# A hybrid decoder layer: conditioning pieces placed by columns given to TensorE, a third score buffer, later attention products

## The chip, the cores and the metric

The kernel runs on one core of a Trainium2 chip. The metric is the device time of one execution in microseconds (us). TensorE is called PE, VectorE DVE, ScalarE ACT, GpSimd POOL and SyncE SP. DMA transfers are issued by SP and POOL.

## The reference

One layer of a decoder on x (512 tokens by 2048), with a conditioning vector c of 2048 that is turned into 24 vectors of 512 values each (scales, shifts and gates):

```
mod = c_act @ wm                               # 24 groups of 512 columns, 2048 deep
h = rms_norm(x) * (1 + scale1) + shift1
h @ w_in -> group A: windowed attention, 16 query heads, 2 key/value heads, bias, sinks
            group B: 16 heads over 256 latent values; keys chosen per query by a ReLU indexer, top 128
x += gate1 * (concat(out_A, out_B) @ w_out)
h = rms_norm(x) * (1 + scale2) + shift2
x += gate2 * W_down(silu(causal_dwconv3(W_u h)) * (W_g h))       # 5632 wide
out = rms_norm(x)
```

Everything is float32.

## The kernel before

Activations lie transposed, features on 128 partitions and 512 tokens along a row. A float32 product is made of three passes in a shorter format: weights and activations are split into a high part (ACT, L129) and a low part (DVE, L130), and `mm3` (L133 to L136) gives TensorE high by high, high by low and low by high. Each 128 x 128 block of weights is thus three matmuls of 512 columns.

The projections are cut into *units* of 128 output columns, and a unit into four *slots* of 128 x 512 weights, which are 12 matmuls. `drive` (L315 to L329) goes through the slots: it starts loads five slots ahead on SP, splits three ahead, gives the slot's matmuls, and then calls `step` (L249). A step advances every active Python generator to its next `yield`, so that their work lies between the slots. Something that was put on the list `middle` is run by `run_middle` (L243) in the middle of the next slot's matmuls, or at the start of the next step. The order in which Python gives instructions sets priorities; the framework then puts each engine's stream in an order of its own by these and by its estimates, and each engine works its stream off in that order, waiting where an input is not there.

The stages, in the time of the trace: 0 to 190 us keys, values and index projection; 190 to 360 the units qa0 to qa7 (queries of group A) with the indexer, the top-k (L641 to L649: names gt, isc, cnt, wk) and pairs of A heads; 360 to 575 the units qb0 to qb7 (queries of B) with pairs of B heads; 575 to 796 the output projection, units wo0 to wo15, with x loaded in four parts of 1 MB (x2, used at L908); 796 to 2212 the gated MLP.

*A pair of heads* (`pair_gen`) goes step by step: score matmuls into PSUM (sca, scb), the bias and row minimum on DVE (L726, into a tile s, from a tag with two buffers), exp on ACT (L728), the division (`norm`), then `turns(p)`, which transposes four 128 x 128 blocks of each head into a bank (tag tp, two banks; L748) and copies it to et on ACT (L749), and `product(p)` (L762), which multiplies et by the values. A head of A has two such parts, one of B three. Before each pair of B heads, `prep_gen` makes keys from a 128 x 256 slice of wuk (names wuk0h/l to wuk7h/l): matmuls into kbp, which takes one of the two tp banks until `dup_k` (L563 to L566) has copied it to kb with two ACT and two DVE operations.

*Conditioning.* Groups 0 to 7 of mod come first. The rest is done by `mod_gen`: a *piece* is a 256 KB load and one DVE operation on 128 x 512 values that adds a row block times c to macc (L183). After 16 pieces, four small matmuls (mps, L193) sum macc over partitions, and the bias is added a step later (L230). Groups 8 to 13 run beside qb, four pieces a step, with five buffers, loaded by POOL; 14 to 19 beside wo, three a step, eight buffers, loaded by POOL (L1238); 20 to 23 beside the MLP, two a step, five buffers, loaded by SP.

Of the kernel before, what the change touches and what calls it, by code (L numbers as in the profile page):

```python
# [8 lines left out]
F32 = mybir.dt.float32  # L9
# [24 lines left out]
def hybrid_trunk(ctx, tc, xT, cT, wm, bm, nrm, wik, wiq, wi1, sinks, kvn, wuk, wuv, rel, onehot,  # L34
# [3 lines left out]

    const = ctx.enter_context(tc.tile_pool(name="const", bufs=1))
# [202 lines left out]

    def run_middle():  # L243
        todo = list(middle)
        middle.clear()
        for f in todo:
            f()

    def step():  # L249
        run_middle()  # L250
        for group in (active, idle):
            for g in list(group):
                if next(g, StopIteration) is StopIteration:
                    group.remove(g)

    def finish_all():
        while active or idle or middle:
            step()
# [56 lines left out]
    def drive(slots, lo, hi):  # L315
        for i in range(lo, hi):
# [4 lines left out]
            if middle:  # L321
                slots[i].mm(slots[i].w, range(2))
                run_middle()
                slots[i].mm(slots[i].w, range(2, 4))
            else:
                slots[i].mm(slots[i].w)
# [329 lines left out]
    ka = p1.tile([P, 4, T], F32R, name="ka")  # L656
# [29 lines left out]


    class Head:
# [10 lines left out]

        def load(self):  # L700
            self.nt = self.tb_src.shape[-1]
            self.tb = p1.tile([P, T], F32, tag="tb", bufs=2, name=f"tb{self.name}")
            sp.dma_start(self.tb[:, :self.nt], self.tb_src)

        def scores(self):
            name, spans = self.name, self.spans
            s = self.s = p1.tile([P, 1280], F32, tag="s", bufs=2, name=f"s{name}")
# [44 lines left out]
    def pair_gen(heads, o_of, done):  # L752
# [23 lines left out]
        middle.append(lambda: turns(1))  # L776
        yield
        product(0)
        product(1)
        if len(heads[0].parts) > 2:  # L780
            turns(2)
            middle.append(lambda: (product(2), done()))
            yield
        else:
            done()
# [414 lines left out]
    drive(slots, 0, marks["qb0"] - 4)  # L1200
    start(prep_gen(0))
    drive(slots, marks["qb0"] - 4, marks["qb0"])
    while idle:
        step()
    start(mod_gen(range(8, 14), ring_mod, 5, p1, sc_ps, 4), low=True)
    drive(slots, marks["qb0"], marks["wo"])
# [12 lines left out]
    for i in range(6):  # L1219
# [3 lines left out]
        drive(slots, marks["wo"] + i, marks["wo"] + i + 1)  # L1223
# [17 lines left out]
    start(mod_gen(range(14, 20), px_mod, 8, px, o_bank, 3), low=True)  # L1241
    at = marks["wo"] + 6
    for i in range(1, 4):
        n = (1,1,4)[i - 1]
        drive(slots, at, at + n)
        sp.dma_start(env["x2"][i], xT[i])
        at += n
    drive(slots, at, marks["ff"])
# [20 lines left out]
    start(mod_gen(range(20, 24), ring_mod, 5, p2, o_bank, 2), low=True)  # L1269
# [97 lines left out]
```

## Time and profile before

| | us |
|---|---|
| median of 3 runs | 2205.24 (2204.67 to 2207.21) |
| profiled execution, its own time | 2213.56 |
| its span, first to last instruction | 2211.8 |
| PE busy | 2149.8 (97%) |
| DVE busy | 1567.8 (71%) |
| ACT busy | 975.8 (44%) |
| POOL busy | 242.2 (11%) |

The profile is of one execution. Busy time counts matmuls, element-wise operations and the like, not waits. Bracketed at the end of a row of the timeline is the idle time of that engine before the row and what ended it. The granted clock (PEclk) is a share of TensorE's full 2.4 GHz; it is at full or at half of that, and a value between is a mean. An x and a number is the count of instructions in a row.

### The profile page before, as it was taken

The page shows a single profiled execution, that of the slowest core. Times are in us where ns is not written, and L with a number is a line of the kernel's source. Part 1 is how long each engine was busy: PE and PEld are TensorE (multiplying, and loading weights), DVE is VectorE, ACT ScalarE, POOL GpSimd, SP SyncE. Part 2 cuts the span into 40 slices and gives each one's busy share as a digit, 9 for nine tenths or more (in the row PEclk, how much of TensorE's full clock was granted, in tenths as well). Part 3 has the DMA queues.
Part 4 walks back from the last instruction along what each step waited for, and adds up shares of the span by engine and source line. Part 5 has one row for each costly group of instructions (what it writes and reads, how often), then busy time and mean ns, then how long its engine had stood idle before and what let it go on. Part 6 is the DMA issues. An engine that isn't in the chain of part 4 may idle for free.

```text
span 2211.8 us, 30173 instructions
## 1 busy us (share of the span) xinstructions
PE 2149.8 (97%) x10376; PEld 1752.7 (79%) x10376; DVE 1567.8 (71%) x2829; ACT 975.8 (44%) x1850; POOL 242.2 (11%) x376
## 2 busy tenths in 40 slices
PE   8999999998989999999999999999999999999997
PEld 4777777777768888888888888888888888888887
DVE  2887999787679576975757676665857666675766
ACT  4334876676722263434333343334333343334332
POOL 0000000222034000000101010110201010110200
PEclk9999999999999999999999999999999999999999
DMA  9783321666499436744737465564727465563672
GB/s 384 271 288 113 107 72 56 201 219 212 151 359 343 150 127 189 253 148 120 161 95 169 113 147 133 133 145 118 163 92 166 119 140 140 131 148 114 120 251 77
DMA packets 168921, 367.09 MB, mean 166 GB/s; under 512 B 20159, under 2 KB 27343, under 8 KB 162624
## 3 DMA queue, kind: packets, MB, share of 16 engines
q1 hardware_dynamic: 130208, 270.81, 37.3%
q0 software_dynamic: 37696, 92.79, 19.9%
q8 instruction: 81, 1.33, 0.2%
q10 hardware_dynamic: 864, 1.57, 0.2%
q14 instruction: 72, 0.59, 0.1%
HBM read 312.93 MB, written 52.17 MB: 165 GB/s over the span
## 4 chain that ended last, share of the span: by engine, by line
PE 72%; issue 17%; DMA 5%; POOL 2%; DVE 2%; ACT 1%; SPq 0%; POOLq 0%; DVEq 0%; ACTq 0%
PE p L1053 6%; PE p L1055 6%; PE p L1054 6%; DMA mraw<-in_wm_dram 4%; POOL mraw L1238 1%; POOL mraw L123 1%; PE qip L134 1%; PE mrow L188 1%; PE qip L135 1%; PE qip L136 1%; DMA xn<-in_xT_dram 0%; DVE macc L183 0%; PE mps L193 0%; DMA wiq<-in_wiq_dram 0%; PE cT L1105 0%
## 5 line engine op out<-in xcount | busy, mean ns | idle before, releaser
L169 ACT CAST dh<-rq 128x512 fp32r<-128x512 f32 x240 | 149.5, 623 | 182.9 <-PE p L1055 145.5
L183 DVE SCALAR_TENSOR_TENSOR macc<-mraw,cact,macc 128x512 f32<-128x512 f32 x240 | 179.6, 748 | 26.2 <-DMA mraw<-in_wm_dram 22.5
L170 DVE TENSOR_TENSOR dl<-rq,dh 128x512 fp32r<-128x512 f32 x240 | 160.9, 686 | 43.8 <-ACT dh L169 42.9
L1053 PE MATMUL p<-dh,ah 128*128 128x512 f32 x480 | 187.0, 390 | 0.0
L1055 PE MATMUL p<-dh,al 128*128 128x512 f32 x480 | 186.9, 389 | 0.0
L1054 PE MATMUL p<-dl,ah 128*128 128x512 f32 x480 | 186.9, 389 | 0.0
L1064 POOL DMA_DIRECT2D cd<-co x72 | 61.4, 858 | 875.0 <-DVE co L1077 872.6
L1053 PEld LDWEIGHTS p<-dh,ah 128*128 128x128 f32 x480 | 90.2, 188 | 18.7
L1054 PEld LDWEIGHTS p<-dl,ah 128*128 128x128 f32 x480 | 90.1, 188 | 18.7
L1055 PEld LDWEIGHTS p<-dh,al 128*128 128x128 f32 x480 | 90.1, 188 | 18.7
L123 POOL DMA_DIRECT2D mraw<-in_wm_dram x96 | 51.6, 538 | 357.6 <-DVE macc L181 131.1
L1080 DVE TENSOR_TENSOR v<-p,v 128x512 f32<-128x512 f32 x120 | 82.3, 686 | 6.0 <-PE p L1055 5.2
L1064 POOL DMA_DIRECT2D cd<-v x72 | 61.4, 856 | 128.1 <-DVE v L1082 76.1
L1238 POOL DMA_DIRECT2D mraw<-in_wm_dram x96 | 51.4, 536 | 133.4 <-DVE nmb L726 53.7
L170 DVE TENSOR_TENSOR al<-cu,ah 128x256 fp32r<-128x256 f32 (+2 forms) x60 | 46.7, 779 | 23.9 <-ACT ah L169 21.2
L169 ACT CAST ah<-cu 128x256 fp32r<-128x256 f32 (+2 forms) x60 | 41.5, 692 | 49.4 <-DVE cu L979 25.9
L1077 DVE TENSOR_TENSOR co<-p,v 128x512 f32<-128x512 f32 x80 | 54.9, 686 | 6.7 <-PE p L1055 6.7
L999 DVE TENSOR_TENSOR rq<-rq,rq 128x512 f32<-128x512 f32 x80 | 52.4, 684 | 0.0
L479 DVE TENSOR_TENSOR qi<-qi,qip 128x512 f32<-128x512 f32 x56 | 38.3, 684 | 14.4 <-PE qip L136 13.7
L170 DVE TENSOR_TENSOR dl_t<-tw,dh_t 128x512 fp32r<-128x512 f32 x40 | 27.7, 692 | 22.9 <-ACT dh_t L169 22.9
L728 ACT ACTIVATE sb<-sb,nmb 128x512 f32<-128x512 f32 (+2 forms) x64 | 35.3, 552 | 13.3 <-DVE nmb L726 13.0
L378 DVE SCALAR_TENSOR_TENSOR macc<-mraw,cact,macc 128x512 f32<-128x512 f32 x54 | 40.3, 746 | 0.4
(4498 smaller groups left out, 6447.5 us busy)
## 6 DMA issues: line engine op xcount, KB each, us to landing
mraw<-in_wm_dram POOLq DMA_DIRECT2D x192, 256.0 KB, 5.6
rq<-in_wdn_dram SPq DMA_DIRECT2D x160, 256.0 KB
mraw<-in_wm_dram SPq DMA_DIRECT2D x32, 1024.0 KB
cd<-co POOLq DMA_DIRECT2D x80, 256.0 KB, 4.6
cd<-v POOLq DMA_DIRECT2D x80, 256.0 KB, 4.6
mraw<-in_wm_dram SPq DMA_DIRECT2D x64, 256.0 KB
wiq<-in_wiq_dram SPq DMA_DIRECT2D x32, 256.0 KB
wik<-in_wik_dram SPq DMA_DIRECT2D x8, 592.0 KB
```

The lines of the kernel that those rows point to most:

```text
L123: by.dma_start(t, src)
L169: act.copy(hi_t, full)
L170: dve.tensor_tensor(lo_t, full, hi_t.bitcast(F32), OP.subtract)
L183: dve.scalar_tensor_tensor(acc, t, cact[:, kt:kt + 1], acc, OP.mult, OP.add)
L999: dve.tensor_tensor(self.b[out], self.b[a], self.b[b], OP.add)
L1053: pe.matmul(ps[b], ah[:, tok], wh, start=k == 0, stop=False)
L1054: pe.matmul(ps[b], ah[:, tok], wl, start=False, stop=False)
L1055: pe.matmul(ps[b], al[:, tok], wh, start=False, stop=k == 1)
L1064: pool.dma_start(cd[tb][dq], t, accum_op=OP.add)
L1077: dve.tensor_tensor(t, ps, box["v" if i == 1 else "u", b], OP.subtract)
L1080: dve.tensor_tensor(box["v", b], ps, box["v", b], OP.add)
L1238: pool.dma_start(t, wm[g, kt // 4][:, kt % 4])
```

## The change

A wrapper, `Counted`, takes TensorE's place in the kernel and adds up, while the program is built, the columns of each matmul and transpose (four times as many for float32 data, half for outputs on 64 partitions). `pace` puts a generator on a list with a number of columns, and `run_paced`, called at the end of each step and, with `halves=True`, in the middle of each slot, advances it once for each such number that TensorE has been given. `mod_gen` now yields after each piece. The numbers are 5200 for groups 8 to 13, 3500 for 14 to 19 and 20000 for 20 to 23. `finish_all` gives what is left of a paced generator at once.

`Head.third` lets every third B head use ka's buffer (A's keys, free by then) for its tile s, beside the two buffers of tag s. In `pair_gen`, the last product of an A pair moves to the middle of the following slot; for a B pair the second transposes move from the middle of a slot to behind the first product, the second product and the third transposes to the middle of the next slot, and the third product one step on. As the wrapper gives all matmuls of the changed kernel, they have its line (L53, transposes L57) in the orders below.

```diff
--- before.py
+++ after.py
@@ -36,6 +36,27 @@
     nc = tc.nc
     act, dve, pe, pool, sp = nc.scalar, nc.vector, nc.tensor, nc.gpsimd, nc.sync
 
+    class Counted:
+
+        def __init__(self, to):
+            self.to, self.cols = to, 0
+
+        def count(self, out, x):
+            n = 1
+            for d in out.shape[1:]:
+                n *= d
+            n = 4 * n + 22 if x.dtype == F32 else n + 32
+            self.cols += n // 2 if out.shape[0] == 64 else n
+
+        def matmul(self, out, w, x, **kw):
+            self.count(out, x)
+            return self.to.matmul(out, w, x, **kw)
+
+        def transpose(self, out, x, eye):
+            self.count(out, x)
+            return self.to.transpose(out, x, eye)
+
+    pe = Counted(pe)
     const = ctx.enter_context(tc.tile_pool(name="const", bufs=1))
     ring = ctx.enter_context(tc.tile_pool(name="ring", bufs=1))
     big = ctx.enter_context(tc.tile_pool(name="big", bufs=1))
@@ -240,6 +261,19 @@
             yield from gen
         (idle if low else active).append(run())
 
+    paced = []
+
+    def pace(gen, every):
+        paced.append([gen, every, pe.cols])
+
+    def run_paced(all_of=False):
+        for e in list(paced):
+            while all_of or pe.cols >= e[2]:
+                e[2] += e[1]
+                if next(e[0], StopIteration) is StopIteration:
+                    paced.remove(e)
+                    break
+
     def run_middle():
         todo = list(middle)
         middle.clear()
@@ -252,8 +286,10 @@
             for g in list(group):
                 if next(g, StopIteration) is StopIteration:
                     group.remove(g)
+        run_paced()
 
     def finish_all():
+        run_paced(True)
         while active or idle or middle:
             step()
 
@@ -312,15 +348,16 @@
 
         return [Slot(raw, s, mm(s), (lambda: after(box["ps"])) if s == 3 else None) for s in range(4)]
 
-    def drive(slots, lo, hi):
+    def drive(slots, lo, hi, halves=False):
         for i in range(lo, hi):
             for j in range(i, min(i + AHEAD_LOAD + 1, len(slots))):
                 slots[j].load()
             for j in range(i, min(i + AHEAD_SPLIT + 1, len(slots))):
                 slots[j].split()
-            if middle:
+            if halves:
                 slots[i].mm(slots[i].w, range(2))
                 run_middle()
+                run_paced()
                 slots[i].mm(slots[i].w, range(2, 4))
             else:
                 slots[i].mm(slots[i].w)
@@ -653,7 +690,7 @@
     ch = p1.tile([P, 2, T], F32R, name="ch")
     cl = p1.tile([P, 2, T], F32R, name="cl")
     va = p1.tile([P, NB, P], F32, name="va")
-    ka = p1.tile([P, 4, T], F32R, name="ka")
+    ka = p1.tile([P, 4, T], F32R, tag="ka", bufs=1, name="ka")
     wit = tmp_t("wit", (16, T))
     dup_k(ki_ps[0:64], 0, ki[:, 0], ki[:, 1])
     act.mul(wit, ki_ps[64:80], 1.0 / 32.0)
@@ -684,6 +721,8 @@
             split_to(ch[:, i], cl[:, i], cf[i])
         yield
 
+    turn_s = [0]
+
 
     class Head:
 
@@ -697,6 +736,13 @@
             self.parts = [jobs[g:g + 4] for g in range(0, len(jobs), 4)]
             self.ets = {}
 
+        def third(self):
+
+            if len(self.parts) < 3:
+                return False
+            turn_s[0] += 1
+            return turn_s[0] % 3 == 0
+
         def load(self):
             self.nt = self.tb_src.shape[-1]
             self.tb = p1.tile([P, T], F32, tag="tb", bufs=2, name=f"tb{self.name}")
@@ -704,7 +750,11 @@
 
         def scores(self):
             name, spans = self.name, self.spans
-            s = self.s = p1.tile([P, 1280], F32, tag="s", bufs=2, name=f"s{name}")
+            if self.third():
+                s = p1.tile([P, 1280], F32, tag="ka", name=f"s{name}", padded_shape=[P, 4 * T])
+            else:
+                s = p1.tile([P, 1280], F32, tag="s", bufs=2, name=f"s{name}")
+            self.s = s
             nm = p1.tile([P, NB], F32, tag="nm", bufs=3, name=f"nm{name}")
             den = self.den = p1.tile([P, NB], F32, tag="den", bufs=3, name=f"den{name}")
             banks, used, where = [], [], [None] * NB
@@ -773,15 +823,19 @@
         heads[1].norm()
         yield
         turns(0)
-        middle.append(lambda: turns(1))
-        yield
-        product(0)
-        product(1)
-        if len(heads[0].parts) > 2:
-            turns(2)
-            middle.append(lambda: (product(2), done()))
+        if len(heads[0].parts) == 2:
+            middle.append(lambda: turns(1))
+            yield
+            product(0)
+            middle.append(lambda: (product(1), done()))
             yield
         else:
+            yield
+            product(0)
+            turns(1)
+            middle.append(lambda: (product(1), turns(2)))
+            yield
+            product(2)
             done()
 
     mixa = {}
@@ -1197,13 +1251,13 @@
 
     start(ahead(index_gen(), 0))
     start(ahead(keys_gen(), 0))
-    drive(slots, 0, marks["qb0"] - 4)
+    drive(slots, 0, marks["qb0"] - 4, True)
     start(prep_gen(0))
-    drive(slots, marks["qb0"] - 4, marks["qb0"])
+    drive(slots, marks["qb0"] - 4, marks["qb0"], True)
     while idle:
         step()
-    start(mod_gen(range(8, 14), ring_mod, 5, p1, sc_ps, 4), low=True)
-    drive(slots, marks["qb0"], marks["wo"])
+    pace(mod_gen(range(8, 14), ring_mod, 5, p1, sc_ps, 1), 5200)
+    drive(slots, marks["qb0"], marks["wo"], True)
     env["mh"] = mh = big.tile([P, KT, T], F32R, tag="b2", name="mh")
     env["ml"] = ml = big.tile([P, KT, T], F32R, tag="b3", name="ml")
 
@@ -1220,7 +1274,7 @@
         if i < 3:
             for kt in range(4 * i, 4 * i + 4):
                 mix_in(kt)
-        drive(slots, marks["wo"] + i, marks["wo"] + i + 1)
+        drive(slots, marks["wo"] + i, marks["wo"] + i + 1, True)
     finish_all()
     for kt in range(12, 16):
         mix_in(kt)
@@ -1238,14 +1292,14 @@
         pool.dma_start(t, wm[g, kt // 4][:, kt % 4])
         return t
 
-    start(mod_gen(range(14, 20), px_mod, 8, px, o_bank, 3), low=True)
+    pace(mod_gen(range(14, 20), px_mod, 8, px, o_bank, 1), 3500)
     at = marks["wo"] + 6
     for i in range(1, 4):
         n = (1,1,4)[i - 1]
-        drive(slots, at, at + n)
+        drive(slots, at, at + n, True)
         sp.dma_start(env["x2"][i], xT[i])
         at += n
-    drive(slots, at, marks["ff"])
+    drive(slots, at, marks["ff"], True)
     finish_all()
 
     rs_ps = norm_rows("rs2")
@@ -1266,7 +1320,7 @@
     pxc.__exit__(None, None, None)
     pdc = tc.tile_pool(name="ph4", bufs=1, reuse_waits="tile")
     env["pd"] = pdc.__enter__()
-    start(mod_gen(range(20, 24), ring_mod, 5, p2, o_bank, 2), low=True)
+    pace(mod_gen(range(20, 24), ring_mod, 5, p2, o_bank, 1), 20000)
     drive(slots, marks["ff"] + 12, marks["join"])
     pdc.__exit__(None, None, None)
     env["pe"] = pe2 = ctx.enter_context(tc.tile_pool(name="ph5", bufs=1, reuse_waits="tile"))
```

Each engine has as many instructions as before, of the same kinds and shapes, and POOL's are in the same order. Three places, before and then changed.

The first is on DVE, between the last unit of qa and qb0. isc, gt, cnt and wk (L641 to L646, now L678 to L683) belong to the top-k, sa (L726, now L776) to a head of A, and qb0r_3l is the low half of the weights of qb0's last slot:

```order
L738 RECIPROCAL dena_3601<-dena_3601 128x4
L641 TENSOR_SCALAR gt_3724,cnt_3723<-isc_1632,top_2825 128x512
L130 TENSOR_TENSOR qb0r_3l<-qb0r_3409,qb0r_3h 128x512
L642 TENSOR_SCALAR isc_1632<-isc_1632,top_2825 128x512
L643 TENSOR_SCALAR cnt_3723<-cnt_3723 128x1
L130 TENSOR_TENSOR qb1r_0l<-qb1r_3478,qb1r_0h 128x512
L644 SCALAR_TENSOR_TENSOR wk_2826<-isc_1632 128x512
L130 TENSOR_TENSOR qb1r_1l<-qb1r_3733,qb1r_1h 128x512
L646 SCALAR_TENSOR_TENSOR isc_1632<-wk_2826,cnt_3723,isc_1632 128x512
```

In the changed kernel the same stretch, up to the row behind qb0r_3l:

```order
L679 TENSOR_SCALAR isc_1632<-isc_1632,top_2825 128x512
L680 TENSOR_SCALAR cnt_3715<-cnt_3715 128x1
L776 ISA sa_3637,nma_3638<-sca_1_3645,tba_3548,nsink 128x256
L776 ISA nma_3638 128x1
L681 SCALAR_TENSOR_TENSOR wk_2826<-isc_1632 128x512
L776 ISA sa_3637,nma_3638<-sca_1_3645,tba_3548,nsink 128x128
L776 ISA nma_3638 128x1
L683 SCALAR_TENSOR_TENSOR isc_1632<-wk_2826,cnt_3715,isc_1632 128x512
L151 TENSOR_TENSOR qb0r_3l<-qb0r_3401,qb0r_3h 128x512
L787 TENSOR_TENSOR dena_3639<-dena_3639,esa_3658 128x4
```

qb0r_3l stood behind gt; it now stands behind the chain of gt, isc, cnt and wk up to the second isc, and no split stands between these any more.

The second is on PE in the unit qb2: the transposes of a B pair into tp banks (tpb_0 the first part, tpb_1 the second) and its first product, o from etb. Before:

```order
L134 MATMUL qb2ps<-h1h,qb2r_1h 128x512
L748 MATMUL tpb_0_4101<-identr,sb_3978 128x128 x4
L748 MATMUL tpb_1_4136<-identr,sb_3914 128x128 x4
L135 MATMUL qb2ps<-h1l,qb2r_1h 128x512
L748 MATMUL tpb_1_4143<-identr,sb_3978 128x128 x4
L136 MATMUL qb2ps<-h1h,qb2r_1l 128x512
L762 MATMUL o_4156<-etb_0_4095,vb_3531 64x128
```

Changed, first the transposes of the first part and what follows them:

```order
L53 MATMUL qb2ps<-h1h,qb2r_1l 128x512
L57 MATMUL tpb_0_4049<-identr,sb_3938 128x128 x4
L53 MATMUL qb2ps<-h1h,qb2r_1h 128x512
L53 MATMUL qb2ps<-h1l,qb2r_1h 128x512
L53 MATMUL qb2ps<-h1h,qb2r_1l 128x512
L53 MATMUL o_4084<-etb_0_4043,vb_3531 64x128
```

Seven products on, the end of the first product and what follows it:

```order
L53 MATMUL o_4084<-etb_0_4050,vb_3531 64x128
L57 MATMUL tpb_1_4093<-identr,sb_3882 128x128 x4
L57 MATMUL tpb_1_4100<-identr,sb_3938 128x128 x4
L53 MATMUL scb_0_4110<-kb_4003,qb_4018 128x512
L53 MATMUL scb_0_4110<-keep_3731,identr 128x512
```

The second part's transposes stood directly behind those of the first, two banks one after the other; they now come behind three more matmuls and the first product, and the scores of the next head (scb) follow them.

The third is on DVE at the slice wuk6, whose low half wuk6l the kbp matmuls need; macc is a piece of conditioning, sb belongs to a head's scores. In the kernel before:

```order
L726 ISA sb_5400,nmb_5401<-scb_1_5407,tbb_5261 128x128
L726 ISA nmb_5401 128x1
L183 SCALAR_TENSOR_TENSOR macc_0_5359<-mraw_10_5435,cact,macc_0_5359 128x512
L183 SCALAR_TENSOR_TENSOR macc_0_5359<-mraw_11_5438,cact,macc_0_5359 128x512
L130 TENSOR_TENSOR wuk6l<-wukr_5352,wuk6h 128x256
L738 RECIPROCAL denb_5402<-denb_5402 128x4
L183 SCALAR_TENSOR_TENSOR macc_0_5359<-mraw_12_5480,cact,macc_0_5359 128x512
```

In the changed kernel, with the head's scores in the rows ahead:

```order
L776 ISA sb_5225,nmb_5226<-scb_1_5232,tbb_5174 128x384
L776 ISA nmb_5226 128x1
L776 ISA sb_5225,nmb_5226<-scb_1_5232,tbb_5174 128x128
L776 ISA nmb_5226 128x1
L788 RECIPROCAL denb_5227<-denb_5227 128x4
L151 TENSOR_TENSOR wuk6l<-wukr_5250,wuk6h 128x256
```

Two pieces stood between the scores and wuk6l, and now none. The pieces of group 13 lay in this unit; those of group 12 now lie in the next one, most of them ahead of wuk7l.

## Rows read from the trace of the kernel before

**Rows 1.** The page: the span, and busy time by engine.

```profile
span 2211.8 us, 30173 instructions
...
PE 2149.8 (97%) x10376; PEld 1752.7 (79%) x10376; DVE 1567.8 (71%) x2829; ACT 975.8 (44%) x1850; POOL 242.2 (11%) x376
```

**Rows 2.** Stretches: their length, then each engine's busy time, clock, DMA share, GB/s.

```profile
360.00:560.00 200.00, 181.00 (x1108) 146.79 (x1107) 155.47 (x356) 135.03 (x326) 40.79 (x76) 0.95 0.58 183
560.00:640.00 80.00, 69.28 (x395) 56.19 (x394) 57.25 (x113) 46.44 (x105) 12.29 (x23) 0.95 0.70 245
640.00:740.00 100.00, 98.65 (x435) 80.94 (x436) 86.98 (x139) 25.49 (x41) 38.62 (x72) 0.96 0.88 309
740.00:800.00 60.00, 58.40 (x285) 48.78 (x284) 25.68 (x42) 20.64 (x32) 0.00 (x0) 0.99 0.36 119
800.00:2130.00 1330.00, 1330.00 (x5907) 1101.88 (x5906) 900.51 (x1426) 519.61 (x841) 131.44 (x160) 1.00 0.57 146
```

**Rows 3.** Waits of PE, 360 to 800 us: in total, times, longest.

```profile
PE tpb L748 <- ACT etb L749: 9.1, 6, 3.4
PE mps L193 <- DVE macc L183: 6.8, 2, 5.5
PE tpa L748 <- ACT sa L741: 4.7, 2, 3.3
PE wo0ps L134 <- ACT mh L169: 2.9, 2, 2.6
PE kbp L136 <- DVE wuk6l L130: 2.4, 1, 2.4
PE kbp L136 <- DVE wuk5l L130: 2.0, 1, 2.0
PE wo0ps L135 <- DVE ml L170: 1.4, 1, 1.4
PE kbp L134 <- ACT wuk6h L129: 0.6, 1, 0.6
```

**Rows 4.** Line L183 on DVE, 360 to 800 us: durations (ns), idle time before.

```profile
L183 DVE SCALAR_TENSOR_TENSOR macc<-mraw,cact,macc x180: 723/751/754, 395.3 to 732.8; 128x512 f32<-128x512 f32 x180
...
  DMA mraw<-in_wm_dram: 21.5, 21
```

**Rows 5.** Timeline of DVE, about 414 us: start, busy, line, operation.

```profile
414.09 0.75 DVE L183 SCALAR_TENSOR_TENSOR macc<-mraw,cact,macc 128x512 f32<-128x512 f32 x1 [1.57 <-DMA mraw<-in_wm_dram]
414.76 0.68 DVE L565 TENSOR_TENSOR kb<-kbp,kb 64x512 fp32r<-64x512 f32 x1
```

**Rows 6.** Timeline of DVE, about 542 us.

```profile
542.15 0.75 DVE L183 SCALAR_TENSOR_TENSOR macc<-mraw,cact,macc 128x512 f32<-128x512 f32 x1 [1.81 <-DMA mraw<-in_wm_dram]
542.82 0.42 DVE L130 TENSOR_TENSOR wuk6l<-wukr,wuk6h 128x256 fp32r<-128x256 f32 x1
```

**Rows 7.** Timeline of PE, 543 to 550 us.

```profile
543.30 0.80 PE L136 MATMUL kbp<-ch,wuk6l 128*128 128x512 f32 x1 [2.38 <-DVE wuk6l L130]
543.89 0.63 PE L134 MATMUL kbp<-ch,wuk6h 128*128 128x512 f32 x1
...
549.71 0.39 PE L136 MATMUL qb7ps<-h1h,qb7r_0l 128*128 128x512 f32 x1
```

**Rows 8.** Timeline of DVE, 386 to 391 us.

```profile
386.70 0.68 DVE L130 TENSOR_TENSOR qb0r_3l<-qb0r,qb0r_3h 128x512 fp32r<-128x512 f32 x1
...
390.08 0.74 DVE L646 SCALAR_TENSOR_TENSOR isc<-wk,cnt,isc 128x512 f32<-128x512 f32 x1
```

**Rows 9.** Timeline of PE, about 387 us.

```profile
386.91 0.84 PE L748 MATMUL tpa<-identr,sa 128*128 128x128 f32 x3 [1.44 <-ACT sa L741]
```

**Rows 10.** Timeline of DVE, about 622 us.

```profile
622.03 0.75 DVE L908 SCALAR_TENSOR_TENSOR x<-wo0ps,mod,x 128x512 f32<-128x512 f32 x1 [5.41 <-DMA x<-in_xT_dram]
```

**Rows 11.** Timeline of PE, about 638 us.

```profile
638.27 1.84 PE L193 MATMUL mps<-ones,macc 128*128 128x1 f32 x8 [5.49 <-DVE macc L183]
```

## The prediction

> **What bounds the kernel now.** I read the page's engine table first: TensorE (PE) is busy for 2149.8 of 2211.8 us, VectorE (DVE) 71%, and the other engines less [rows 1]. The kernel is bound by TensorE, so a reordering can win only TensorE's idle time, 62 us, and the time that it runs at half rate. The table of stretches says where those lie [rows 2]. From 800 to 2130 us TensorE is busy for all of 1330.00 us at a clock of 1.00: 5907 records, 0.225 us a matmul. Nothing is to be had there. From 360 to 800 us, where the change works, it is idle for 19.0, 10.7, 1.35 and 1.6 us, and the clock is 0.95, 0.95, 0.96 and 0.99. A granted clock below 1 is work not done: (1 − clock) × length is 10.0 + 4.0 + 4.0 + 0.6 = 18.6 us at most, part of it in idle time.
>
> The table of waits names who ends TensorE's waits between 360 and 800 us [rows 3]: transposes into a "tp" bank that wait for ScalarE (ACT) to copy out the one before (9.1 us in 6 waits), conditioning sums "mps" that wait for their last piece on DVE (6.8 in 2), transposes of A heads (4.7), the first wo0 matmul (2.9), kbp that waits for the low half of a wuk slice on DVE (2.4 and 2.0), wo0 on ml (1.4). 29.3 us in all.
>
> Behind several stands the same thing. The conditioning pieces run on DVE in order with everything else, 751 ns each, and in this stretch they held DVE idle 21 times, 21.5 us, because their DMA hadn't landed [rows 4]. What stands behind them is late. At 414.09 a piece waited 1.57 us, and the kb split behind it started at 414.76 [rows 5]; ScalarE's queue stood waiting for that kb, with the et copy behind it, and the transposes waited 3.4 us. At 542.15 a piece waited 1.81 us and wuk6l came at 542.82 [rows 6]; the kbp matmul waited 2.38 us until 543.30 [rows 7]. After such a stall matmuls run for a while 0.63 us long instead of 0.39, about 0.43 apart: the lower level, 1.2 instead of 2.4 GHz. From 543.30 to 549.71 there are 15 spacings, 6.41 us, where 15 × 0.225 = 3.4 would do: 3.0 us on top of the stall [rows 2, 7].
>
> **The change part by part.** All instructions stay, with the same shapes; only the order changes, and POOL's not at all. So no duration is added, and the sum is over waits. The profiled execution took 2213.56 us, 8.3 above the median of 2205.24; I work out a difference there and take it off the median.
>
> *Pieces by columns, groups 8 to 13.* A step gave four pieces at once; now one comes per 5200 columns. The 32 slots of B's projections took some 215 us, 6.7 a slot, so the 24 steps' fours become about three a slot, spread over half slots.
> - wuk6l (third place in the order below): only two pieces stand before it in its unit, and the two late ones directly ahead are gone. Wait 2.38 + half rate 3.0 + the 0.6 behind wuk6h ahead of it: +6.0 if all goes, 0 if another piece takes the place. I take +6.0, since the nearest stands ten rows ahead of it.
> - 418.50 (second place): no pieces stand on DVE from 390 us until after this kb, and the second transposes come a step later, behind the first product. ScalarE's own queue of kb and qb copies stays, some 1.8 us. Wait 3.4 − 1.8, and about 1.1 of half rate: +2.7 (0 to 5.1).
> - The five other tp waits, 9.1 − 3.4 = 5.7 us: the one of 2.1 keeps its pieces in front; of the others I take 1.9 as won (0 to 3.6).
> - wuk5l: its 2.0 us goes, and the turn behind it becomes later by about as much with a half-rate stretch: −0.7 (−2.7 to +2.0).
> - 386.91 (first place): TensorE waited 1.44 us for sa, and found qb0r_3l done, since DVE started it at 386.70 and its 0.68 us were over [rows 8, 9]. Now qb0r_3l stands behind the scan and the last isc operation of the top-k. That one starts at 390.08 and lasts 0.74; three splits of 0.62 spacing no longer stand in front of it, so qb0r_3l starts at about 389.0, some 2.3 later, and with the score operations that now stand between up to 390. qb1 matmuls that could have filled the time come behind it too. Wait 2.7 to 3.5, and half rate after it about 2 as in [rows 7]: −5.5 (−7 to −1).
> - wuk7l: in before no piece stood in that unit ahead of it, now 13 to 15 do. 14 × 0.75 = 10.5 us of DVE in a unit of 27 us, of which DVE was idle for 22%, 6 us [rows 2]. The rest, 4.5, is late or was early enough: between nothing and a stall like wuk6l's, 2.4 + 3.0. The wo0 wait of 2.6 us behind it lies partly in the same time. Half of the upper end: −2.5.
> - Group 13's last pieces are flushed before slot 6 of wo: twelve stand before the last ml, where there were eight. 4 × 0.75 = 3.0 beyond a wait that was there already (1.4); some of it hides behind wo1's other matmuls: −2 (−3 to 0).
>
> *Groups 14 to 19, per 3500 columns.* At 622.03 DVE waited 5.41 us for x2's DMA, with pieces behind it, and mps waited 5.49 at 638.27 [rows 10, 11]. Group 20's loads, which stood ahead of x2's on SP's queue, come later, and mps now stands 18 rows later on TensorE, 18 × 0.225 = 4 us; about 15 pieces and 7 splits (22 × 0.66 = 14.5 us) stand between x and mps, where it was 13 and 6. So a wait of about 2.5 stays: +3.0, and of the clock's 4.0 us in 640 to 740 I give 2 to this place: +5.0 (0 to 7.5). The second mps wait, 6.8 − 5.5 = 1.3, and the other 1.7 of the clock go, because there the pieces come with room to spare and mps stands six matmuls into the next unit: +3.0 (0 to 3.0).
>
> *Groups 20 to 23, per 20000 columns.* Their pieces now spread over the stretch where TensorE is never idle: 0. DVE covers it, with 900.51 busy of 1330 [rows 2]; without that cover 64 × 0.75 = 48 us would be exposed.
>
> *The third place for scores.* TensorE waits for no place of s: in [rows 3] no score bank has a row. 0, with 0.5 either way. *Halves in drive:* the order of matmuls in a slot stays; 0.
>
> Sum: 6.0 + 2.7 + 1.9 − 0.7 − 5.5 − 2.5 − 2.0 + 5.0 + 3.0 = 7.9 us faster. The profiled execution would be 2205.7; from the median 2197.3, I say 2197. Its own range is 2190 to 2204.
>
> In the stretch with products and transposes through two tp banks the clock is 0.95, and in the long stretch of projections, which also changes banks all the time, 1.00 [rows 2]; each half-rate stretch I looked at starts behind a stall, as in [rows 7]. The Trainium skill, "TensorE: Matmul & The Clock Gate", section "A second HAM failure mode: psum-queue depth-cycling", says otherwise of one kernel: cycling through PSUM banks makes TensorE idle briefly between groups so often that its clock swings. By that rule turns and products cut into smaller pieces would make the half rate worse, and the sum would be what rival 4 gives; by the row, nothing is lost.
>
> **The rivals.**
> 1. *A piece stands late in front of each wuk slice: slower.* DVE is in order and five buffers feed the pieces, so an even pace could put a late one in front of wuk's low half in every unit. For it: wuk5l and wuk6l were hit [rows 3], pieces waited 21 times [rows 4], wuk7l now has pieces ahead. Against: fewer come at once. One hit costs 2.4 + 3.0 = 5.4. The sum has half of one; two more turn it to +2.9 lost, three more to 8.3 lost. It decides from two hits above the sum: 2208 to 2214, middle 2211.
> 2. *The stalls move along: no change.* The 418 and tp waits and wuk6l's reappear at the next transposes and slices, since ScalarE's copies and the two tp banks stay: the sum without 6.0 + 2.7 + 1.9 is 2.7 lost, 2208. For it: the wait of 2.1 has its pieces in front in both orders; against: the places differ by ten pieces.
> 3. *All of it goes.* tp 9.1, mps 6.8, kbp 5.0 (2.4 + 2.0 + 0.6) and half of the clock's 18.6, less wuk7l and ml 4.5: 25.7 us, 2180. For it: all three have pieces ahead. Against: sa's wait stays, and the first place costs.
> 4. *The clock swings more.* A second 0.05 on the 200 us, 10.0 us [rows 2]: 2197.3 + 10.0 = 2207. Against: the row of 1.00.
>
> **How the numbers follow.** Forecast 0.52, rival 1 0.17, rival 2 0.20, rival 3 0.08, rival 4 0.03. A measurement here tells 0.2%, 4.4 us, from no change: below 2200.8 is faster, above 2209.7 slower. Faster: 0.45 of the forecast's and 0.08 of rival 3, 0.53. Slower: 0.12 of rival 1, 0.05 of rival 2 and 0.01 of rival 4, 0.18. Same: the rest, 0.29. The range leaves out rival 3 (0.08) and the upper end of rival 1 (about 0.08): 2186 to 2212.
>
> **What would show it.** Right: no kbp wait of over 1 us at the sixth slice, and full-rate matmuls behind it; the waits of tp below 5 us in all; the mps wait of 5.5 at 2 to 3; a new wait of 2 to 3.5 us on qb0r_3l near 388 us; a clock of 0.97 or more from 560 to 740. 800 to 2130 us is as long as before. Wrong: kbp waits in several units, ScalarE's copies ending waits of tp as long as before, an x wait of 5 us still in front of mps, or a difference that lies behind 800 us.

## The result and the profile after

The changed kernel takes 2219.51 us (median of 5 runs, 2216.74 to 2221.85) against 2205.67 of before beside it: 1.0059 of before, 95% interval 1.0044 to 1.0073. It is 13.8 us slower by the two medians, where 7.9 us faster was forecast, and the time lies outside the range.

The page and the table of stretches of the changed kernel, to set beside [rows 1, 2]:

```profile
span 2220.1 us, 30149 instructions
...
PE 2149.7 (97%) x10376; PEld 1750.1 (79%) x10376; DVE 1568.2 (71%) x2829; ACT 976.2 (44%) x1850; POOL 242.4 (11%) x376
```

```profile
360.00:560.00 200.00, 179.25 (x1085) 144.07 (x1084) 137.18 (x328) 134.10 (x325) 28.98 (x54) 0.96 0.47 143
560.00:640.00 80.00, 72.23 (x403) 56.87 (x403) 60.29 (x115) 45.36 (x103) 20.34 (x38) 0.94 0.72 253
640.00:740.00 100.00, 89.23 (x398) 74.00 (x397) 79.35 (x126) 24.06 (x39) 32.71 (x61) 0.93 0.91 318
740.00:800.00 60.00, 59.72 (x289) 50.01 (x288) 40.02 (x67) 17.79 (x28) 9.65 (x18) 1.00 0.65 218
800.00:2130.00 1330.00, 1327.64 (x5890) 1099.49 (x5888) 898.96 (x1422) 523.06 (x844) 131.43 (x160) 1.00 0.57 144
```

TensorE's busy time is the same to 0.1 us as in that profile of before, which lay 8 us above its median. A second profile of before, of the same order on every engine (experiment 12, 2206.88 us), reads:

```profile
span 2205.1 us, 30173 instructions
...
PE 2142.4 (97%) x10376; PEld 1746.7 (79%) x10376; DVE 1567.2 (71%) x2829; ACT 975.8 (44%) x1850; POOL 242.4 (11%) x376
```

Against it the changed kernel is 15.0 us longer: TensorE is idle for 7.7 us more, and busy for 7.3 us more with the same instructions, at a granted clock of 0.987 over the span where it was 0.990: (1 − clock) × span is 28.9 us against 22.1. So about half of the loss is waiting, and half is longer busy time at the lower level of the clock. From 640 to 740 us TensorE was idle for 1.35 us and now is for 10.8 (the wait of mps, which lay just before 640 in [rows 11], lies in this stretch now); DMA in 740 to 800 went from 0.36 to 0.65. TensorE's waits in the changed kernel from 360 to 820 us (total, times, longest), for [rows 3]:

```profile
PE mps L53 <- DVE macc L204: 12.2, 2, 10.8
PE tpb L57 <- ACT etb L799: 8.7, 6, 2.6
PE tpa L57 <- ACT sa L791: 4.9, 2, 2.9
PE o L53 <- ACT etb L799: 4.3, 2, 2.5
PE wo0ps L53 <- ACT mh L190: 3.3, 1, 3.3
PE kbp L53 <- DVE wuk7l L151: 3.0, 1, 3.0
PE qb0ps L53 <- DVE qb0r_3l L151: 2.3, 1, 2.3
```

The waits on wuk5l and wuk6l are gone, as is the second mps wait of 1.3. New are o on et, wuk7l and qb0r_3l, and the longest wait of mps has doubled, from 5.5 to 10.8 us. The timeline of DVE shows what ends that one:

```profile
644.91 0.74 DVE L204 SCALAR_TENSOR_TENSOR macc<-mraw,cact,macc 128x512 f32<-128x512 f32 x1
652.66 1.42 DVE L204 SCALAR_TENSOR_TENSOR macc<-mraw,cact,macc 128x512 f32<-128x512 f32 x2 [7.01 <-DMA mraw<-in_wm_dram]
```

and TensorE behind it:

```profile
643.07 0.39 PE L53 MATMUL wo3ps<-mh,wo3r_3l 128*128 128x512 f32 x1
...
654.23 1.84 PE L53 MATMUL mps<-ones,macc 128*128 128x1 f32 x8 [10.77 <-DVE macc L204]
```

The two operations at 652.66 are, by DVE's order (names with their numbers), the sixth piece of group 20 and the last of group 14:

```order
L204 SCALAR_TENSOR_TENSOR macc14_0_6145<-mraw14_14_6235,cact_99,macc14_0_6145 128x512
L204 SCALAR_TENSOR_TENSOR macc20_0_7961<-mraw20_5_8017,cact_99,macc20_0_7961 128x512
L204 SCALAR_TENSOR_TENSOR macc14_0_6145<-mraw14_15_6250,cact_99,macc14_0_6145 128x512
```

Group 20 had been through at 612 us before, ahead of x2's loads. Its pieces use the same five buffers as groups 8 to 13; as group 13 now ends at 619 us, group 20 starts at 621, and its loads stand on SP among those of wo in a stretch where DMA is full (410 GB/s from 620 to 650). Group 14's last piece stands behind one that nobody needs before 800 us. The two loads, group 20's on SP and group 14's on POOL, were given at

```profile
640.82 0.43 SPq L144 DMA_DIRECT2D mraw<-in_wm_dram  x1
637.52 0.54 POOL L1292 DMA_DIRECT2D mraw<-in_wm_dram  x1 [0.18 <-issue]
```

By the trace's record group 14's had landed at 645.05 us. Without the piece in front, its operation could have followed the one at 644.91; the 7.01 us of waiting and 0.67 for the other piece are thus about 7.7 of the 10.77 us (an estimate from these rows).

By the starts of the units' first matmuls, in us:

| stretch | before again | changed | no third place (13) | paces alone, 4200 (8) | paces alone, 5200 (16) | that, held (17) |
|---|---|---|---|---|---|---|
| qb0 to wo0 | 215.9 | 220.7 | 212.6 | 213.6 | 210.0 | 209.3 |
| wo0 to wo2 | 39.2 | 45.0 | 47.5 | 39.2 | 41.7 | 41.3 |
| wo2 to wo4 | 32.5 | 36.3 | 25.5 | 28.3 | 37.2 | 31.9 |
| wo4 to wo10 | 70.7 | 67.2 | 68.8 | 67.2 | 67.3 | 67.2 |
| wo10 to u0 | 75.1 | 76.8 | 76.8 | 76.8 | 76.8 | 80.3 |
| ratio to before, timed | 1 | 1.0059 | 0.9988 | 0.9971 | 1.0004 | 0.9998 |

From u0 to the end of the span the six take 1415.4 to 1417.8 us. Each column is one execution. The 15.0 us between the first two columns are 1.6 before qb0, 4.8, 5.8, 3.8, −3.5 and 1.7 in the rows of the table, and 0.8 behind u0.

### The profile page after: what moved, and what is told of

Its sections match the earlier page's. It is cut to its first block, busy times and chain, and to the rows that moved or that the text cites. A ratio compares the mean times of both kernels' runs of the same rounds, so it can differ in the third digit from the quotient of the medians.

```text
span 2220.1 us, 30149 instructions
## 1 busy us (share of the span) xinstructions
PE 2149.7 (97%) x10376; PEld 1750.1 (79%) x10376; DVE 1568.2 (71%) x2829; ACT 976.2 (44%) x1850; POOL 242.4 (11%) x376
## 4 chain that ended last, share of the span: by engine, by line
PE 79%; issue 13%; DMA 4%; DVE 2%; POOL 1%; ACT 1%; SPq 0%; POOLq 0%; DVEq 0%; ACTq 0%
PE p L53 17%; PE qip L53 3%; DMA mraw<-in_wm_dram 3%; POOL mraw L144 1%; PE ckv L53 1%; PE mps L53 1%; PE mrow L53 1%; DMA wiq<-in_wiq_dram 1%; DVE macc L204 1%; PE d_2ps L53 1%; PE u0ps L53 1%; PE g0ps L53 1%; PE d_0ps L53 1%; PE d_1ps L53 1%; PE wo15ps L53 0%
## 5 line engine op out<-in xcount | busy, mean ns | idle before, releaser
L53 PE MATMUL p<-dh,ah 128*128 128x512 f32 x480 | 186.7, 389 | 0.0
L53 PE MATMUL p<-dl,ah 128*128 128x512 f32 x480 | 186.7, 389 | 0.0
L53 PE MATMUL p<-dh,al 128*128 128x512 f32 x480 | 186.7, 389 | 0.0
L53 PEld LDWEIGHTS p<-dh,al 128*128 128x128 f32 x480 | 90.2, 188 | 18.7
L53 PEld LDWEIGHTS p<-dh,ah 128*128 128x128 f32 x480 | 90.1, 188 | 18.7
L53 PEld LDWEIGHTS p<-dl,ah 128*128 128x128 f32 x480 | 90.0, 188 | 18.8
L778 ACT ACTIVATE sb<-sb,nmb 128x512 f32<-128x512 f32 (+2 forms) x64 | 35.3, 554 | 24.9 <-DVE nmb L776 21.4
```

The source lines that it names most:

```text
L53: return self.to.matmul(out, w, x, **kw)
```

## The experiments

Diffs are against the changed kernel. By *pairs as before* stands this (B, then A):

```diff
-            yield
+            middle.append(lambda: turns(1))
+            yield
             product(0)
-            turns(1)
-            middle.append(lambda: (product(1), turns(2)))
-            yield
-            product(2)
-            done()
+            product(1)
+            turns(2)
+            middle.append(lambda: (product(2), done()))
+            yield
...
-            middle.append(lambda: (product(1), done()))
-            yield
+            product(1)
+            done()
```

**1, a faster pace.**

```diff
-    pace(mod_gen(range(8, 14), ring_mod, 5, p1, sc_ps, 1), 5200)
+    pace(mod_gen(range(8, 14), ring_mod, 5, p1, sc_ps, 1), 4200)
```

> The changed kernel with one number altered: groups 8 to 13 get a piece per 4200 columns instead of 5200. Then group 13 is through ahead of wuk7l, and group 20, which uses the same five buffers, is through before the last slot group of wo2, as in the kernel before. Theory A (the pace of 5200 is too slow: group 13 runs on into wo0 and wo1 and pushes group 20 into the stretch where DMA is full; one of group 20's pieces then stands late in front of group 14's last): the wait of mps near 650 us falls from 10.8 to 2 to 5.5 us, no piece of group 20 stands between group 14's, and the time is 2204 to 2212. The wait of kbp on wuk7l (3.0 us) stays under both theories, since 16 pieces stand in front of it. Theory B (the later products and transposes of B pairs cost the time): 2215 to 2221.

Measured: 1.0024 (1.0011 to 1.0037). The wait of mps is 4.3 us. Better than 1.0059, but a loss is left: 2212.72 us, just above theory A's range and below theory B's.

**2, the first pace alone.** Pairs as before, and:

```diff
-    pace(mod_gen(range(14, 20), px_mod, 8, px, o_bank, 1), 3500)
+    start(mod_gen(range(14, 20), px_mod, 8, px, o_bank, 3), low=True)
...
-    pace(mod_gen(range(20, 24), ring_mod, 5, p2, o_bank, 1), 20000)
+    start(mod_gen(range(20, 24), ring_mod, 5, p2, o_bank, 2), low=True)
...
-            return turn_s[0] % 3 == 0
+            return False
```

> The kernel before, with the pace of 5200 columns for groups 8 to 13 alone; groups 14 to 23, the pairs and the places for scores as before. Theory A: group 13 is flushed in wo1, group 20 lies among groups 14 to 17, and the time is 2213 to 2222; a wait of mps of 5 us or more between 630 and 670. Theory B: 2203 to 2209.

Measured: 0.9998 (0.9986 to 1.0009), with a wait of mps of 8.7 us. Its 2207.75 us are in theory B's range. The slow pace by itself loses nothing against before: in the profile it wins 8.6 us from qb0 to wo0 (207.3 against 215.9) and loses 5.7 from wo0 to wo4, so theory A falls as the whole cause.

**3, pairs and third place alone.** All three `pace` lines back to `start` with 4, 3 and 2 a step.

> The kernel before, with the new order of products and transposes and the third place for scores alone; all conditioning by steps. Theory A: 2201 to 2208, with mps waiting near 638 us as before. Theory B: 2213 to 2221, with waits of o on et and of the transposes above the 9.1 us of before by 6 or more.

Measured: 1.0024 (1.0013 to 1.0036). 2214.06 us, the lower end of theory B: a loss that no pace explains. The waits for et (o and transposes) are 12.1 us, though, 3 above the 9.1 of before, where theory B asked for 6.

**4, groups 8 to 13 by steps.**

```diff
-    pace(mod_gen(range(8, 14), ring_mod, 5, p1, sc_ps, 1), 5200)
+    start(mod_gen(range(8, 14), ring_mod, 5, p1, sc_ps, 4), low=True)
```

> The changed kernel with groups 8 to 13 by steps again (four a step); groups 14 to 23 by columns, pairs and score places as changed. Theory A: the loss goes and what the rest brings is seen alone: 2199 to 2208, no wait on wuk7l, a mps wait near 640 us of at most 5.5. Theory B: 2213 to 2221.

Measured: 1.0018 (1.0004 to 1.0032). 2214.6 us, theory B's range, but with the signs of theory A: no wait on wuk7l, and 4.1 us at mps. Of the changed kernel's loss of 5.9 permille (thousandths; one is 2.2 us) 1.8 stay without the slow pace, and 4.1 go with it.

**5, the A pairs' edit alone.** All else undone.

> The kernel before, with one edit: the last product of an A pair goes to the middle of the next slot. Theory C (this edit alone moves qb0r_3l behind the top-k chain, and the wait of 2.3 us with the half rate behind it is what the pairs cost): 1.0015 to 1.003 of before, 3 to 7 us slower, with the wait on qb0r_3l near 385 us. Theory D (the B pairs' later products cost it): within 0.001 of before.

Measured: 0.9997 (0.9979 to 1.0014), though the new wait is there, next to a tpa wait that got shorter by 0.8 us (4.7 before):

```profile
PE tpa L57 <- ACT sa L791: 3.9, 2, 2.9
PE qb0ps L53 <- DVE qb0r_3l L151: 2.3, 1, 2.3
```

Theory C falls.

**6, A pairs as before.**

> The changed kernel with the A pairs' last product where it was before; everything else as changed. Theory C: the wait on qb0r_3l goes, and the time is 1.002 to 1.004 of before instead of 1.0059. Theory D: 1.005 to 1.007, whether the wait goes or not.

Measured: 1.0037 (1.0022 to 1.0052). That is theory C's range, and the wait on qb0r_3l is gone. In this company the edit is worth 2.2 permille, 5 us; the two intervals (1.0044 to 1.0073 for the changed kernel) overlap.

**7, B pairs as before.**

> The changed kernel with the B pairs' steps as before; A pairs, places for scores and all paces as changed. Theory C: 1.005 to 1.007 of before, as the changed kernel. Theory D: 1.000 to 1.003, with the waits of o on et gone and the transposes' waits on et below 5 us.

Measured: 0.9991 (0.998 to 1.0003): theory D, and further than it said; the waits of o are gone, those of the transposes are 5.7 us. It also has group 14's last piece ahead of group 20's sixth, and a wait of mps of 2.9 us.

**8, the paces alone, at 4200 columns.** Pairs as before, 4200 as in 1, `third` returns False.

> The changed kernel with pairs and places for scores as before, so all conditioning by columns, and groups 8 to 13 at 4200 columns instead of 5200. If the losses are the pairs' (5 us) and the late group 20's (8 us), and the paces otherwise win what was forecast of them in the stretch of qb, this one is 0.995 to 0.999 of before, 2 to 11 us faster, with a mps wait near 640 us of at most 5 us. If the paces win nothing: 0.999 to 1.002.

Measured: 0.9971 (0.9958 to 0.9983), 2200.31 us against 2207.72. It beats both kernels.

**9 and 18, groups 20 to 23 held back.**

```diff
+    cuse[0] = const.tile([P, KT], F32, name="cactb")
+    dve.scalar_tensor_tensor(cuse[0], a2, 0.0, cact, OP.mult, OP.add)
     pace(mod_gen(range(20, 24), ring_mod, 5, p2, o_bank, 1), 20000)
```

(`mod_acc` takes its scalars from `cuse[0]`.)

> The changed kernel, but groups 20 to 23 use a copy of c's values that is made from a2, which is there only after group 19; so no piece of theirs can stand among groups 14 to 19 (one small DVE operation more). DVE's order up to wo1 is the changed kernel's. If the piece of group 20 in front of group 14's last one costs what the two waits of mps suggest (10.8 us against 2.9 where the two stand the other way round), the wait of mps falls to 2 to 4 us and the time to 1.0015 to 1.003 of before, 6 to 10 us below the changed kernel. If DMA traffic as such makes that wait, it stays at 6 us or more and the time at 1.004 to 1.006.

> The changed kernel with groups 20 to 23 held back once more (e9 gave four runs between 2215 and 2224, too wide to tell 6 us). If group 20's piece costs the changed kernel what its wait shows: 1.002 to 1.0045 of before. If what is won at mps is lost elsewhere: 1.005 to 1.007.

Measured: 1.0062 (1.004 to 1.0084) and 1.0059 (1.0041 to 1.0078). The mps wait fell from 10.8 to 3.4 and 5.0 us, and the medians not at all. The profile of 9, the fastest of its four runs (2215.22 us), does have the gain, 27.9 us from wo2 to wo4 where the changed kernel has 36.3; that of 18 has 32.4.

**10, B pairs at 4200.** Experiment 8 with the B pairs' new order.

> The paces alone with 4200 columns (which took 0.9971 of before) and the B pairs' new order on top; A pairs and score places as before. Theory D (the B pairs' new order costs the time): 1.001 to 1.003, with waits of o on et that the paces alone don't have. If it is rather the A pairs' edit or the third place for scores: 0.996 to 0.999.

Measured: 0.9984 (0.9974 to 0.9993). The waits that this order was charged with are not there without the third place:

```profile
PE o L53 <- ACT etb L799: 0.7, 2, 0.4
PE tpb L57 <- ACT etb L799: 0.3, 1, 0.3
```

Others are there in their place: 8.8 us on slices of wuk, and 3.4 of scores on qb. From qb0 to wo0 TensorE is idle for 21.4 us (20.4 in experiment 8), and the stretch is 217.1 us long, 3.5 more than there, at a granted clock of 0.95 against 0.97.

**11, B transposes as before, later products kept.**

```diff
-            yield
+            middle.append(lambda: turns(1))
+            yield
             product(0)
-            turns(1)
             middle.append(lambda: (product(1), turns(2)))
```

> The changed kernel at 4200 columns (1.0024 of before), with a B pair's second transposes in the middle of the slot ahead of the first product, as before; the later second and third products stay. Theory D1 (the transposes behind the first product leave the copies to ScalarE no time, so o waits for et): 0.997 to 1.000, without waits of o on et of over 1 us. Theory D2 (the pair that takes a step longer costs it): 1.0015 to 1.003.

Measured: 1.004 (1.0024 to 1.0055). D1 falls: the waits of o on et did go, but those of the transposes on et rose to 14.5 us. This order is no better than the changed one, and 1.004 is above D2's range too.

**12, all undone.**

> The changed kernel's text with every edit undone, which gives the kernel before's order on every engine: 0.998 to 1.002 of before under any theory. It is for its profile, since the one profiled execution of before lay 8 us above the median: here 2200 to 2212.

Measured: 2206.88 us in its one run, as expected, with the waits of [rows 3] (tpb 9.3, mps 6.6, wuk6l 2.1).

**13, no third place for scores.**

```diff
-            return turn_s[0] % 3 == 0
+            return False
```

> The changed kernel without the third place for scores; paces (5200), A pairs and B pairs as changed. Theory T (the third place is what makes the new B order lose: with it the transposes wait for et 8.7 us and o for et 4.3, and in the B order without it, at 4200, 0.3 and 0.7): those waits fall below 3 us in all, and the time to 0.999 to 1.003 of before instead of 1.0059. Theory D (B pairs' order by itself): 1.005 to 1.007.

Measured: 0.9988 (0.9976 to 1.0001), 7.1 permille or 16 us below the changed kernel by this one line. The waits for et fell to 2.0 us, as theory T said; others came up:

```profile
PE mps L53 <- DVE macc L204: 5.2, 2, 3.4
...
PE kbp L53 <- DVE wuk2l L151: 2.9, 1, 2.9
PE qb0ps L53 <- DVE qb0r_3l L151: 2.3, 1, 2.3
...
PE scb L53 <- DVE qb L587: 2.0, 2, 1.6
...
PE tpb L57 <- ACT etb L799: 1.4, 2, 1.1
```

The line has a second effect: by DVE's order group 20's sixth piece no longer stands in front of group 14's last one, whose mps waits 1.8 us here.

**14, no third place, 4200.**

> The same with 4200 columns: A and B pairs and all paces as changed, no third place. Theory T: 0.998 to 1.0005 (the B pairs and paces at 4200 took 0.9984, and the wait on qb0r_3l of the A pairs comes on top), against 1.0024 with the third place. Theory A2 (the A pairs' edit costs 4 permille at this pace): 1.0015 to 1.003.

Measured: 0.9999 (0.9988 to 1.0011), against 1.0024 with it (1), and 0.9984 without the A pairs' edit (10).

**15, paces at 4200 and the third place.** Experiment 8 with `third` as changed.

> All paces at 4200 (0.9971 of before) with the third place, pairs as before. If the third place costs by itself: 1.000 to 1.003. If it costs only together with the new order of B pairs: 0.996 to 0.9985.

Measured: 0.9979 (0.997 to 0.9989). With the old order of pairs the third place costs 0.8 permille, less than the intervals can tell.

**16, the paces alone at 5200.** Experiment 8 with the changed kernel's number.

> All paces as changed (5200, 3500, 20000), pairs and score places as before. Against the same at 4200 (0.9971) it tells what the slow pace alone costs: if the late groups 13 and 20 cost what the waits of mps suggest, 0.9995 to 1.002; if they cost nothing, 0.9965 to 0.998.

Measured: 1.0004 (0.9994 to 1.0013), 3.3 permille or 7 us above 4200. Its wait of mps and that of experiment 8, both from 600 to 820 us:

```profile
PE mps L53 <- DVE macc L204: 12.0, 2, 11.6
```

```profile
PE mps L53 <- DVE macc L204: 3.0, 1, 3.0
```

**17, that, with groups 20 to 23 held.**

> The paces alone at 5200 columns (1.0004 of before, with a wait of mps of 11.6 us), with groups 20 to 23 held back as in e9. If a piece of group 20 in front of group 14's last one is what costs the difference between 5200 and 4200 columns: mps waits 2 to 5 us and 0.9965 to 0.9985. If not: 0.9995 to 1.001.

Measured: 0.9998 (0.9987 to 1.0009); its waits from 600 to 820 us:

```profile
PE mps L53 <- DVE macc L205: 5.5, 2, 5.1
PE rs2pssps L53 <- DVE sq_acc L948: 1.9, 1, 1.9
PE u0ps L53 <- ACT h2h L186: 1.4, 1, 1.4
```

The stretch wo2 to wo4 became 5.3 us shorter, and wo10 to u0 3.5 longer, where the norm now waits 1.9 us for its squares (0.2 in experiment 16). In experiment 18 it is 3.9 won and 5.4 lost (32.4 and 82.2 us). Holding group 20 back takes one wait away and makes another at the norm, so this edit can't price the first. Why it makes the second was not followed further.

## Why the prediction was wrong

*Two steps failed, and at 5200 columns they hang together. The first is "the third place for scores: 0".* It was priced by whether TensorE waits for a score tile; it doesn't. What a further place changes, as I read the orders, is how far ahead the next head's work may be put, and with it the order of ScalarE's queue. Together with the new order of B pairs it cost 7.1 permille at 5200 columns (13) and 2.5 at 4200 (1 against 14), with the old order less than can be told (15 against 8). What the two edits together make is waits for et: 10.3 to 13.8 us in all seven orders that have both (changed, 1, 3, 4, 6, 9, 18), 1.0 to 2.0 in those with the B order alone (10, 13, 14), 4.4 to 5.7 in those with the paces and the old order of B pairs, with the third place or without (7, 8, 15, 16, 17).

The 7.1 permille are not this step's alone. In the profiles of the changed kernel and of 13, 8.1 of the 14.9 us of the table lie between qb0 and wo0 and 8.3 between wo0 and wo4, where group 20's piece goes out of the way by the same line (wo4 to wo10 is 1.6 the other way). Undoing the B order (7, 6.8 permille) takes both away too. At 4200 columns that piece is in neither order, and the third place's price is 2.5 permille; there the profiles of 1 and 14 don't show it as waits, for from qb0 to wo0 TensorE is idle for 23.2 us with the third place and without, the waits having moved to wuk and qb (at 5200: 27.0 with it, 20.0 without). So the price is shown by the runs, and its way through the waits for et only at 5200 columns.

Between qb0 and wo0 the rows of ScalarE in the changed kernel, before a wait of the transposes, and that wait on TensorE behind them, read:

```profile
491.60 0.61 ACT L150 CAST qb5r_3h<-qb5r 128x512 fp32r<-128x512 f32 x1
492.11 0.62 ACT L150 CAST wuv4h<-wuvr 128x512 fp32r<-128x512 f32 x1
492.74 0.58 ACT L599 CAST kb<-kbp 64x512 fp32r<-64x512 f32 x1
...
493.81 0.59 ACT L586 ACTIVATE qb<-qb4ps 64x512 fp32r<-64x512 f32 x1
494.43 0.58 ACT L799 COPY etb<-tpb 128x512 f32<-128x512 f32 x1
```

```profile
495.07 0.66 PE L57 MATMUL tpb<-identr,sb 128*128 128x128 f32 x4 [2.49 <-ACT etb L799]
```

and without the third place (experiment 13):

```profile
494.44 0.61 ACT L150 CAST qb5r_3h<-qb5r 128x512 fp32r<-128x512 f32 x1
494.94 0.58 ACT L799 COPY etb<-tpb 128x512 f32<-128x512 f32 x1
495.42 0.62 ACT L150 CAST wuv4h<-wuvr 128x512 fp32r<-128x512 f32 x1
496.07 0.58 ACT L599 CAST kb<-kbp 64x512 fp32r<-64x512 f32 x1
```

The copy that frees the tp bank stands behind the second kb and qb in the one, and ahead of wuv4h and kb in the other. No DMA and no piece is in this wait: the order of one queue is. The two other transposes' waits of over 2 us, at 439.44 and 523.52, also end with a copy ahead of which ScalarE worked without a gap. The two waits of o, 4.3 us, are of another kind. Here is the longer one, on DVE, ScalarE and TensorE:

```profile
524.44 0.75 DVE L204 SCALAR_TENSOR_TENSOR macc<-mraw,cact,macc 128x512 f32<-128x512 f32 x1 [2.60 <-DMA mraw<-in_wm_dram]
526.52 0.58 ACT L599 CAST kb<-kbp 64x512 fp32r<-64x512 f32 x1 [3.05 <-DVE kb L603]
528.85 1.09 PE L53 MATMUL o<-etb,vb 128*64 128x128 f32 x14 [2.47 <-ACT etb L799]
```

A piece waits for its load, the kb splits wait behind it on DVE, ScalarE's kb waits for those, and the copy to et behind kb comes late. That is the chain that the prediction read at 414 us in the kernel before; the one at 444.15 (1.9 us) is the same, behind a piece that waited 2.48 us at 439.75. At the place that the prediction named for it (its 418.50) the wait did fall, from 3.4 to 1.1 us; the stall moved to other pairs.

That the copies' places make the waits is read from these rows; that the third place makes them together with the B order is shown by 7, 10, 13 and 15; why the framework orders ScalarE's queue so is not shown. The forecast's gains on the transposes (2.7 + 1.9) are the same step's other side: 8.7 us of waits stayed and 4.3 on o came, while the order without the third place has 1.4 and 0.6.

*The second step that failed is groups 14 to 19, +5.0.* The wait of mps was forecast to fall to 2.5 us and rose to 10.8. I had group 20's loads out of x2's way and called that a help; I didn't look where they went. They went in front of group 14's last piece. All orders at 5200 with that place (changed, 2, 6, 16) wait 8.7 to 11.6 us, those with group 14 ahead (7, 13) and those at 4200 columns (1, 8, 10, 14, 15) 1.2 to 4.3 us, and 11 5.5. The rows at 652.66 give it about 7.7 us of TensorE's wait. Its price in time is less sure: 16 against 8 gives 3.3 permille or 7 us, with other orders changed besides; 9, 17 and 18 couldn't take it away alone. So neither step is clearly the larger. Where group 20 is through early (8), the step came out as forecast: from wo2 to wo10 95.5 us against 103.2, 7.7 less, with 5.0 + 3.0 in the sum. The 3.0 came in the changed kernel too: wo4 to wo10 is 3.5 us shorter.

*The other steps by their sizes.* qb0r_3l: forecast 2.7 to 3.5 us of wait and 5.5 in all; the wait is 2.3, and the edit behind it cost 5 us in one company (6), 3 in another (10 against 14), both with intervals that overlap, and 0 alone (5): 5.5 was too much. wuk7l: 2.5 forecast, a wait of 3.0. wuk6l, wuk5l and the second mps wait went, as forecast. Groups 20 to 23: 0.8 us behind u0, so 0 was right. The flush of group 13: wo0 to wo2 became 5.8 us longer, 2 were forecast; with the paces alone it is 2.5 at 5200 columns (16) and nothing at 4200 (8), so it is the slow pace's in part.

The sum's gain exists: the paces without the other edits and at 4200 columns took 7.4 us off by the medians (8), where 7.9 had been forecast for all. It is the paces' alone, at a pace the change didn't have, and that the two numbers are close is luck: the 7.9 has 5.5 lost to the A pairs in it. Rival 1 (a late piece in front of each wuk slice) didn't happen in the changed kernel: one slice was hit for 3.0 us and one for 0.4; in 16 three were, for 6.2 together. Rival 2's mechanism, stalls that move along, did happen in part: the waits for et were 9.1 us and are 13.0, and wuk7l took wuk6l's place; its number, 2208, did not. The third place's price and group 20's late piece were in none of the rivals. Rival 4 did not happen: the clock from 360 to 560 us is 0.96 where it was 0.95.

## What to carry to other kernels

Another buffer is no free edit where a scheduler fills in-order queues: the order of every queue can change with it, and what then stands behind what on another engine must be read from the order, not from whether anyone waited for the buffer. A pace set for one group of work moves everything that shares its buffers; follow the last of them to where it now lands and ask which queue and which transfers are full there. One undone edit can take two losses away at once: 13 changed ScalarE's queue and the place of group 20's piece. So undo edits one at a time and also in pairs: here the A pairs' edit alone was worth 0, the third place 0.8 permille beside the old order of pairs, the B order 1.3 without that place, and the three together, with the paces at 4200 columns, 5.3.

## What the runs showed that was not expected

Executions of one kernel lie as far apart as the edits: 31 of before, beside experiments 1 to 4, took 2199 to 2213 us, median 2208. Where half rate sets in differs between two executions of the same order: behind the first matmul after wuk6l's wait the first profile of before had 14 slow ones (nearly all 0.63 us), the second 11; after the transposes' wait of 2.1 us at 443 the first had seven, and after the same wait, 1.9 us, the second none. A single profile tells where the waits are, and not the time to 5 us.
